# A two-layer hybrid decoder trunk on one core: the per-layer embedding's products and additions are set apart within an expert group's turn

## The chip, the cores and the metric

The kernel runs on one core of a Trainium2 chip. TensorE (PE in the profile; PEld is its weight load) multiplies, VectorE (DVE) and ScalarE (ACT) do the elementwise work and empty PSUM, GpSimd (POOL) does little here, and SyncE (SP) issues nearly all transfers. The metric is the device time of one execution in microseconds (us). Three runs of the kernel before took 963.85, 966.4 and 969.9 us; their median, 966.4 us, is the time before.

## The reference

Each of two layers has a token mixer (two kinds of attention) and a channel sublayer. Only the channel sublayer matters here. It works on 256 tokens of 1024 numbers in float32:

```
h   = silu(x W_g[e]) * (x W_u[e])            # 32 experts: 4 groups of 8, D_EXPERT = 256
moe = sum over a token's 2 experts of weight * (h W_d[e])
ple = sigmoid(x @ w_ple_gate) * (p @ w_ple)  # the per-layer embedding: 1024x1024 and 256x1024
x   = layer_norm(ALPHA * x + moe + ple)
```

The embedding `ple` doesn't depend on the experts. It only has to be added to the same sum before the layer norm.

## The kernel before

**The sum.** The output of the channel sublayer, 256 tokens by 1024 columns, stands in four PSUM banks for the whole stage: `ya[t][h]`, with t one of two halves of the tokens (128 each) and h one of two halves of the columns. The residual, the experts' results and the embedding are all added to it by matmuls of TensorE, so that nothing else reads or writes these banks until the layer norm. They are the tiles `acc` in the profile. Four more banks, `mm`, go round for everything else.

**The experts** are worked off in 11 groups (gi = 0 to 10), each of two or four experts whose tokens fill 128 slots in strips of 32. The loop at L1207 to L1231 runs over gi, and in one turn TensorE does, in this order:

- `front(gi + 1)` (L1126): the next group's gate and up products. For each of eight k there are four matmuls, one for each strip of 32 columns of the array, of 512 columns each (`mm<-a,a`, 128*32, in the profile; each matmul has two records, so a front has 32 matmuls and `x64`). ScalarE and VectorE make the activated product `sil` from it (`hidden_act`, L1049).
- `back(gi)` (L1141): this group's down products (`mm<-a,hT`). `halves_of` (L1063) splits them into two fp32r tiles, high by ScalarE (L208) and low by VectorE (L209).
- two gathers of the slots of group gi + 2 (`mm<-gs,a`), from marks that VectorE writes (`marks_of`, L929, one buffer);
- `turned` (L1055): the transposes of `sil` (`mm<-identr,sil`, L95);
- `combine` (L1068): eight matmuls that scatter this group's results into the four sums (`acc<-t,sT`);
- `embeds(gi)` (L1169), in the turns that have one;
- `ways_of` (L935): transposes of the marks (`mm<-identr,gs`) and the slots' weights (`mm<-cw,gs`). VectorE casts the transposes (L919) and copies the weights (L941).

The next turn's `front` follows.

**The embedding** is worked off in quarters of 256 columns (`Embed(q)`, q = 0 to 3) and halves of the tokens, eight units in a layer. One unit (`run(t)`, L741) has three steps:

- `products` (L746): eight matmuls of x and two of p into one `mm` bank, 128 by 256 each (`mm<-a,a` and `mm<-a,pT` with 128*128; two records each);
- `gate` (L759): ScalarE's sigmoid (L762), VectorE's product (L763), then the split into high (ScalarE, L208) and low (VectorE, L209);
- `add` (L768): two matmuls with the identity that add the high and the low part to `ya` (`acc<-t,identr`).

Turn 2 has both units of q = 0 (a part of the first one's products is done before), turns 4 and 5 both of q = 1 and q = 2, turn 6 the first of q = 3 and, in the second layer alone, also the second. In the first layer the last unit is made at the layer's end, by other lines. So 15 of 16 units stand in these turns.

**What sets the order.** The body of the loop is recorded with TensorE's order kept by hand (`manual_schedule`, L1211); the other engines' order comes from a scheduler. Every engine works its instructions off in their order. Weights come by DMA in tiles of 512 KB into an arena of 47 places; SyncE issues each one as soon as its place is free, in a fixed order, far ahead of use.

In turn 3 every engine also reads a count and passes a branch that isn't taken (`leftover`, L1187, in the profile as L1191).

Of the kernel before, what the change touches and what calls it, by code (L numbers as in the profile page):

```python
# [23 lines left out]
DEPTH = 2  # L24
P = 128
KT = D // P
TT = S // P
# [54 lines left out]
def tile_hybrid_trunk(ctx: ExitStack, tc: tile.TileContext, x_in, xT_in, pT_in, pos_in, ws, wik, wrt, lnv,  # L82
# [41 lines left out]
    def bank():  # L124
        return ps.tile([P, 512], F32, tag="mm", bufs=4, name=nm("mm"))

    def wt(shape, dt, tag, bufs):
        return wk.tile(shape, dt, tag=tag, bufs=bufs, name=nm(tag))
# [3 lines left out]
    class Held:  # L132


        def __init__(self, shape, dt=F32, load=False, place=None):
            self.b = arena.take(load, young) if place is None else place
            self.t = wk.tile([P, 1024], dt, tag=f"a{self.b}", bufs=1, name=nm("a"))
            if len(shape) == 2:
                names = "a b"
                self.v = self.t[:, :shape[0] * shape[1]].rearrange("p (a b) -> p a b", a=shape[0])  # L140
            else:
                self.v = self.t[:, :shape[0]]

        def free(self):
            arena.give(self.b)
# [16 lines left out]
    def load(l, i, shape):  # L162
        r = Held(shape, load=True)
        nc.sync.dma_start(r.t, ws[l, i])
        return r
# [19 lines left out]
    def t2(shape, dt=F32):  # L185
        return wt(shape, dt, "t2", t2b)
# [20 lines left out]
    def split(hi, lo, src, eng=V):  # L207
        copied[0] = A.activation(hi, src, AF.Copy)  # L208
        copied[1] = eng.tensor_tensor(lo, src, hi, op=OP.subtract)  # L209
# [124 lines left out]
    def proj(l, first, nk, xs, apart=0, ahead=(), ready=()):  # L334


        o = [acc() for _ in range(TT)]
        late = []

        def mm(t, kt, w):  # L340
            mm3(o[t], xs.get(kt, t), w.v[:, 0, :], w.v[:, 1, :], kt == 0, kt == nk - 1)

        for s in range(nk // 2):
            if not ready:
                r = ahead[s] if s < len(ahead) else load(l, first + s, [2, 512])
            for kt in (2 * s, 2 * s + 1):
                if ready:
                    w = ready[kt]
                elif kt < nk - apart or not ring:
                    w = parts(r.v[:, kt % 2, :], ring if kt < nk - apart else None)  # L350
                else:
                    w = parts(r.v[:, kt % 2, :], [ring.pop(0)])
                mm(0, kt, w)
                if kt < nk - apart:
                    mm(1, kt, w)
                else:
                    late.append((kt, w))
            if not ready:
                r.free()
        for kt, w in late:  # L360
            mm(1, kt, w)
            w.free()
        return o
# [89 lines left out]
    for l in range(DEPTH):  # L453
# [183 lines left out]
        def gate(h, i):  # L637
            g = Held([TT, 512])
            o = proj(l, 28 + 8 * i + 4 * h, KT, xT)
            for t in range(TT):  # L640
                A.activation(g.v[:, t, :], o[t], AF.Sigmoid)
            return g
# [89 lines left out]
        class Embed:  # L732


            def __init__(self, q):
                self.q = q
                self.w = [load(l, O_PLG + 2 * q + k4, [4, 256]) for k4 in range(2)]
                if q % 2 == 0:
                    wple[q // 2] = load(l, O_PLE + q // 2, [4, 256])

            def run(self, t):  # L741
                self.products(t)
                self.gate()
                self.add(t)

            def products(self, t, some=range(KT + 2)):  # L746
# [9 lines left out]
                        PE.matmul(b[:, 256:], pT[:, k - KT, ts], wple[q // 2].v[:, 2 * (q % 2) + k - KT, :], start=False,  # L756
                                  stop=k == KT + 1)

            def gate(self):  # L759
                b = self.b  # L760
                g = wt([P, 256], F32, "sil", silb)
                A.activation(g, b[:, :256], AF.Sigmoid)  # L762
                V.tensor_tensor(g, g, b[:, 256:], op=OP.mult)  # L763
                e = t2([P, 2, 256], F32R)
                split(e[:, 0, :], e[:, 1, :], g)
                self.e = e

            def add(self, t):  # L768
                q, e = self.q, self.e
                yq = ya[t][q // 2][:, (q % 2) * 256:(q % 2 + 1) * 256]  # L770
                for i in range(2):
                    PE.matmul(yq, identr, e[:, i, :], start=False, stop=False)
                if t == TT - 1:
                    free(*self.w)
                    if q % 2:
                        wple[q // 2].free()
# [6 lines left out]
        emb = {0: Embed(0)}  # L783
# [107 lines left out]
        def experts(gi):  # L891

            c = 0
            for r, n, w in groups[gi]:
                for i in range(n):
                    yield r + i, slice(c, c + w)
                    c += w

        def gather(gs, xg, k4):

            b = bank()
            for k in range(4):
                ks = slice((4 * k4 + k) * P, (4 * k4 + k + 1) * P)
                for t in range(TT):
                    PE.matmul(b[:, k * P:(k + 1) * P], x[t].v[:, ks], gs[:, t, :], start=t == 0, stop=t == TT - 1)
            A.activation(xg, b.rearrange("p (k s) -> p k s", k=4), AF.Copy)  # L906
# [28 lines left out]
        def ways_of(gi, gs):  # L935

            sT = wt([P, TT, P], F32R, "sT", 2)
            bw = ways(gs, [cw[:, :, r:r + n] for r, n, w in groups[gi]], sT)
            wsl = wt([P, 1], F32, "wsl", 3)
            for i, (r, sl) in enumerate(experts(gi)):  # L940
                V.tensor_copy(wsl[sl], bw[sl, i:i + 1])  # L941
            return sT, wsl
# [125 lines left out]
        def combine(y, sT, h, t, stop=False):  # L1068

            PE.matmul(ya[t][h], sT[:, t, :], y[0], start=False, stop=False)  # L1070
            PE.matmul(ya[t][h], sT[:, t, :], y[1], start=False, stop=stop)
# [97 lines left out]
        def embeds(gi):  # L1169

            if gi == e1:
                emb[0].products(0, range(wE, KT + 2))
                emb[0].gate()
                emb[0].add(0)
            if gi == e0:
                emb[0].run(1)
            if gi in early:
                q = 1 + early.index(gi)
                if q not in emb:
                    emb[q] = Embed(q)  # L1180
                emb[q].run(0)
                if q < 3:
                    emb[q].run(1)
            if gi == lastat and (l == DEPTH - 1 or lastemb == 2):
                emb[3].run(1)

        def leftover(most):  # L1187
            def onward(cols, n):
# [19 lines left out]
        for gi in range(len(groups)):  # L1208
            if gi == ifat:
                most = nc.values_load(cmi[0:1, 0:1], min_val=0, max_val=S)  # L1210
            here = lambda: tc.manual_schedule(engines={mybir.EngineType.PE})  # L1211
            with here():
                after = front(gi + 1, *slots) if gi < last else None
            if gi == ifat:
                leftover(most)
            with here():
                ys = back(gi, hT)
                if gi + 2 <= last:
                    marks, slots = marks_of(gi + 2), Gathered(gi + 2 >= fg)
                    for k4 in range(2):  # L1220
                        gather(marks, slots.half[k4], k4)
                if gi < last:
                    hT = turned(after[0], wt([P, 2 * P], F32, "hT", hTb))
                    for h in range(2):
                        for t in range(TT):
                            combine(ys[h], sT, h, t)
                    sT = after[1]
                embeds(gi)
                if gi + 2 <= last:
                    slots = slots, *ways_of(gi + 2, marks)  # L1230
            if gi == last - 1:  # L1231
                lng, lnb = wide(2, l), wide(3, l)
                xn = [Held([D]) for _ in range(TT)]
                if l < DEPTH - 1:
                    xT = Split(KT)
# [12 lines left out]
        for t in range(TT):  # L1248
            if t == 1 and l < DEPTH - 1 and lastemb < 2:
                with behind(ends[0] if f1 else None):  # L1250
                    emb[3].gate()
                emb[3].add(1)
            for h in range(2):
                combine(ys[h], sT, h, t, True)
            if t == 0 and l < DEPTH - 1 and lastemb < 2:
                emb[3].products(1)
            with behind((ysplit[1] if o3 else None) if t == 0 else (copied[1] if order2 else None)):
                power = norm.stats(t)
            ends.append(power)
            ends[t:] = [norm.apply(t, o2)]  # L1260
            powers.append(power)
# [76 lines left out]
```

## Time and profile before

| | |
|---|---|
| median of three runs | 966.4 us (963.85 to 969.9) |
| the profiled execution's own time | 968.06 us |
| its span, first to last instruction | 966.5 us |
| mean granted clock of TensorE | 0.987 |
| busy: PE, PEld | 94%, 63% |
| busy: DVE, ACT, POOL | 44%, 36%, 3% |
| transfers | 280.86 MB, mean 291 GB/s |

Busy shares are of the span. A line of the profile names the source line of the helper that records an operation (all matmuls are L92, all transposes by TensorE L95), so operations are told apart by their tiles. The idle time in front of an operation is that of its own engine, with what ended it.

### The profile page before, as it was taken

How to read it: one execution, taken by the hardware profiler on the slowest of the kernel's cores; microseconds unless marked ns; L12 is line 12 of the kernel's file. 1: busy time of each engine (PE TensorE's matmuls, PEld its weight loads, DVE VectorE, ACT ScalarE, POOL GpSimd, SP SyncE). 2: the span in 40 equal slices, each digit the busy share in tenths (PEclk: the TensorE clock that was granted, in tenths of full speed). 3: DMA queues.
4: the chain of work that ended last, by engine and by line, in shares of the span. 5: the costliest groups of instructions: out<-in, count | busy, mean ns of one | idle time of the engine just before them, and what ended most of it. 6: DMA issues, size and time to landing. Idle time of an engine off the chain costs nothing. (4 is left out here: it accounts for less than half of the span.)

```text
span 966.5 us, 15937 instructions
## 1 busy us (share of the span) xinstructions
PE 911.4 (94%) x5761; PEld 605.7 (63%) x5761; DVE 427.8 (44%) x1068; ACT 347.7 (36%) x704; POOL 33.3 (3%) x37
## 2 busy tenths in 40 slices
PE   8999999999998988999799999999999989888994
PEld 5877777785545466544488777787754646456441
DVE  6796566873121211122468864778622121211123
ACT  6557586522111111112346667765121111111120
POOL 0000000100000000000400000001000000000000
PEclk9999999999999999999999999999999999999998
DMA  8994335767899999795997243456869999979933
GB/s 298 408 417 161 125 110 179 261 244 284 320 360 415 388 417 376 310 416 234 397 418 306 88 131 131 139 196 235 305 215 372 378 409 415 399 299 408 370 144 145
DMA packets 79013, 280.86 MB, mean 291 GB/s; under 512 B 9160, under 2 KB 9928, under 8 KB 78928
## 3 DMA queue, kind: packets, MB, share of 16 engines
q1 hardware_dynamic: 78784, 279.78, 76.0%
q8 instruction: 47, 0.77, 0.3%
q14 instruction: 38, 0.31, 0.1%
q10 hardware_dynamic: 144, 0.00, 0.0%
HBM read 278.70 MB, written 1.05 MB: 289 GB/s over the span
## 5 line engine op out<-in xcount | busy, mean ns | idle before, releaser
L92 PE MATMUL acc<-a,a 128*128 128x512 f32 x1440 | 353.2, 399 | 2.1 <-ACT a L208 1.3
L92 PEld LDWEIGHTS acc<-a,a 128*128 128x128 f32 x1440 | 266.0, 189 | 65.1 <-issue 3.2
L92 PE MATMUL mm<-a,a 128*32 128x512 f32 (+5 forms) x1776 | 235.1, 537 | 0.0
L208 ACT ACTIVATE a<-a 128x512 fp32r<-128x512 f32 (+1 forms) x247 | 150.6, 631 | 99.9 <-PE acc L92 69.0
L209 DVE TENSOR_TENSOR a<-a,a 128x512 fp32r<-128x512 f32 (+1 forms) x239 | 161.0, 695 | 50.0 <-ACT a L208 48.6
L92 PEld LDWEIGHTS mm<-a,a 128*32 128x32 f32 (+3 forms) x1776 | 110.7, 132 | 101.4 <-issue 91.1
L92 PE MATMUL mm<-a,hT 128*32 128x512 f32 x704 | 92.2, 604 | 9.0 <-DMA a<-ws 5.0
L92 PEld LDWEIGHTS mm<-gs,a 128*128 128x128 f32 x704 | 80.4, 192 | 17.2 <-PE mm L92 11.7
L92 PE MATMUL mm<-gs,a 128*128 128x128 f32 x704 | 84.7, 278 | 0.0
L1050 ACT ACTIVATE sil<-mm 128x256 f32<-128x256 f32 x22 | 8.4, 383 | 183.2 <-PE mm L92 165.9
L92 PEld LDWEIGHTS mm<-a,hT 128*32 128x32 f32 x704 | 24.3, 111 | 71.5 <-issue 56.5
L1051 DVE SCALAR_TENSOR_TENSOR sil<-sil,wsl,mm 128x256 f32<-128x256 f32 x22 | 10.6, 481 | 131.4 <-ACT sil L1050 131.2
L209 DVE TENSOR_TENSOR t<-mm,t 128x512 fp32r<-128x512 f32 x44 | 30.4, 692 | 68.7 <-ACT t L208 68.7
L208 ACT ACTIVATE t<-mm 128x512 fp32r<-128x512 f32 x44 | 26.3, 597 | 79.0 <-PE mm L92 79.0
L763 DVE TENSOR_TENSOR sil<-sil,mm 128x256 f32<-128x256 f32 x16 | 6.7, 420 | 107.4 <-ACT sil L762 107.4
L92 PE MATMUL acc<-t,sT 128*128 128x512 f32 x176 | 48.8, 413 | 0.0
L906 ACT ACTIVATE a<-mm 128x512 f32<-128x512 f32 x40 | 23.9, 598 | 50.1 <-PE mm L92 50.1
L919 DVE CAST sT<-mm 128x256 fp32r<-128x256 f32 x22 | 9.3, 425 | 69.1 <-PE mm L92 69.1
L92 PEld LDWEIGHTS acc<-t,sT 128*128 128x128 f32 x176 | 31.4, 190 | 9.0 <-issue 2.5
L762 ACT ACTIVATE sil<-mm 128x256 f32<-128x256 f32 x16 | 6.1, 383 | 79.6 <-PE mm L92 79.6
L92 PE MATMUL acc<-t,identr 128*128 128x256 f32 x32 | 12.4, 388 | 21.8 <-ACT t L208 20.6
L548 ACT ACTIVATE t<-mm,mx 128x128 f32<-128x128 f32 (+1 forms) x64 | 26.0, 421 | 10.7 <-DVE mx L545 10.7
(197 smaller groups left out, 648.1 us busy)
## 6 DMA issues: line engine op xcount, KB each, us to landing
a<-ws SPq DMA_DIRECT2D x523, 512.0 KB, 8.4
a<-x_in SPq DMA_DIRECT2D x2, 512.0 KB
out<-a SPq DMA_DIRECT2D x4, 256.0 KB, 2.7
a<-xT_in SPq DMA_DIRECT2D x3, 256.0 KB
a<-wik SPq DMA_DIRECT2D x2, 288.0 KB, 7.6
a<-ws SPq DMA_DIRECT2D x2, 256.0 KB, 4.2
pT<-pT_in SPq DMA_DIRECT2D x2, 256.0 KB
a<-wrt SPq DMA_DIRECT2D x2, 144.0 KB, 2.8
```

What stands on the lines that cost most here:

```text
L92: self.last = nc.tensor.matmul(*a, **k)
L208: copied[0] = A.activation(hi, src, AF.Copy)
L209: copied[1] = eng.tensor_tensor(lo, src, hi, op=OP.subtract)
L548: A.activation(e[:, i * nk:(i + 1) * nk], b[:, i * nk:(i + 1) * nk], AF.Exp, bias=mx[:, i:i + 1], accum_out=sums[i])
L762: A.activation(g, b[:, :256], AF.Sigmoid)
L763: V.tensor_tensor(g, g, b[:, 256:], op=OP.mult)
L906: A.activation(xg, b.rearrange("p (k s) -> p k s", k=4), AF.Copy)
L919: V.tensor_copy(sT, b[:, :2 * P].rearrange("p (t q) -> p t q", t=TT))
L1050: A.activation(sil, gu[:, :FE], AF.Sigmoid)
L1051: V.scalar_tensor_tensor(sil, sil, wsl, gu[:, :FE], op0=OP.mult, op1=OP.mult)
```

## The change

`embeds(gi)` no longer runs the units. It returns a list of them, and the loop calls their three steps at different places of the turn: the first unit's products ahead of `turned`, its gate after `combine`, then the second unit's products and gate, then `ways_of`, and both additions last. `Embed` keeps the gated tiles by t, since two of them are alive now.

```diff
             def __init__(self, q):
-                self.q = q
+                self.q, self.e = q, {}
...
             def run(self, t):
                 self.products(t)
-                self.gate()
+                self.gate(t)
                 self.add(t)
...
-            def gate(self):
+            def gate(self, t):
...
-                self.e = e
+                self.e[t] = e
 
             def add(self, t):
-                q, e = self.q, self.e
+                q, e = self.q, self.e.pop(t)
...
         def embeds(gi):
 
             if gi == e1:
-                emb[0].products(0, range(wE, KT + 2))
-                emb[0].gate()
-                emb[0].add(0)
-            if gi == e0:
-                emb[0].run(1)
+                return [(emb[0], 0, range(wE, KT + 2)), (emb[0], 1, range(KT + 2))]
+            units = []
             if gi in early:
                 q = 1 + early.index(gi)
                 if q not in emb:
                     emb[q] = Embed(q)
-                emb[q].run(0)
-                if q < 3:
-                    emb[q].run(1)
-            if gi == lastat and (l == DEPTH - 1 or lastemb == 2):
-                emb[3].run(1)
+                units = [(emb[q], t, range(KT + 2)) for t in range(TT if q < 3 else 1)]
+            if gi == lastat and l == DEPTH - 1:
+                units.append((emb[3], 1, range(KT + 2)))
+            return units
...
+                units = embeds(gi)
+                for e, t, some in units[:1]:
+                    e.products(t, some)
                 if gi < last:
                     hT = turned(after[0], wt([P, 2 * P], F32, "hT", hTb))
                     for h in range(2):
                         for t in range(TT):
                             combine(ys[h], sT, h, t)
                     sT = after[1]
-                embeds(gi)
+                for e, t, _ in units[:1]:
+                    e.gate(t)
+                for e, t, some in units[1:]:
+                    e.products(t, some)
+                    e.gate(t)
                 if gi + 2 <= last:
                     slots = slots, *ways_of(gi + 2, marks)
+                for e, t, _ in units:
+                    e.add(t)
```

What this does to TensorE's order is shown for turn 4 of the first layer. Here are its rows before, from the last matmul of `combine` on (`mm_3368` and `mm_3387` are the banks of the two units' products, `acc_2072` and `acc_2074` the sums to which they are added, `mm_3407` is `ways_of`, `mm_3453` the front of group 6):

```order
L92 MATMUL acc_2075<-t_640_3329,sT_2856 128x512
L92 MATMUL mm_3368<-a_2309,a_2069 128x256 x4
L92 MATMUL mm_3368<-a_2311,a_2070 128x256 x4
L92 MATMUL mm_3368<-a_2082,pT_1485 128x256 x2
L92 MATMUL acc_2072<-t_649_3382,identr 128x256 x2
L92 MATMUL mm_3387<-a_2309,a_2069 128x256 x4
L92 MATMUL mm_3387<-a_2311,a_2070 128x256 x4
L92 MATMUL mm_3387<-a_2082,pT_1485 128x256 x2
L92 MATMUL acc_2074<-t_652_3401,identr 128x256 x2
L95 MATMUL mm_3407<-identr,gs_3332 128x128 x2
L92 MATMUL mm_3407<-cw_2177,gs_3332 128x2 x2
L92 MATMUL mm_3453<-a_3428,a_3334 32x512 x2
```

Here are TensorE's rows of the change from the same place on (the first unit's products, now `mm_3355`, stand ahead of `turned` and `combine` and so above these rows; the second unit's are `mm_3385`, `ways_of` is `mm_3403`):

```order
L92 MATMUL acc_2075<-t_640_3329,sT_2852 128x512
L92 MATMUL mm_3385<-a_2309,a_2069 128x256 x4
L92 MATMUL mm_3385<-a_2311,a_2070 128x256 x4
L92 MATMUL mm_3385<-a_2082,pT_1485 128x256 x2
L95 MATMUL mm_3403<-identr,gs_3332 128x128 x2
L92 MATMUL mm_3403<-cw_2177,gs_3332 128x2 x2
L92 MATMUL acc_2072<-t_649_3382,identr 128x256 x2
L92 MATMUL mm_3453<-a_3428,a_3334 32x512 x2
L92 MATMUL mm_3453<-a_3439,a_3334 32x512 x2
L92 MATMUL mm_3453<-a_3428,a_3334 32x512
L92 MATMUL acc_2074<-t_652_3399,identr 128x256 x2
L92 MATMUL mm_3453<-a_3428,a_3334 32x512
```

Each addition stood right behind its unit's products. Now the first unit's stands behind `ways_of`, and the second unit's stands in the next group's front, after five of its 32 matmuls: four of k = 0 and the first of k = 1. All eight first units and all seven second units of the two layers stand so.

On VectorE the second unit's gate and `ways_of` are interleaved in the change. Its rows for the same turn are these (`sil_3379` and `t_649_3382` belong to the first unit, `sil_3396` and `t_652_3399` to the second, `gs_3535` are the marks of a later group):

```order
L763 TENSOR_TENSOR sil_3379<-sil_3379,mm_3355 128x256
L209 TENSOR_TENSOR t_649_3382<-sil_3379,t_649_3382 128x256
L919 CAST sT_3402<-mm_3403 128x256
L763 TENSOR_TENSOR sil_3396<-sil_3396,mm_3385 128x256
L941 COPY wsl_3409<-mm_3403 64x1 x2
L929 TENSOR_TENSOR gs_3535<-iom,posm_2178 128x256
L209 TENSOR_TENSOR t_652_3399<-sil_3396,t_652_3399 128x256
```

The low half of the second unit (the last row) stood ahead of the cast, the copies and the marks before, and stands behind them now. Turn 5 has four copies in place of two, and turn 2 no marks at this place. SyncE's transfers keep their order, but two of them pass to the other side of the branch of turn 3.

## Rows read from the trace of the kernel before

**Rows 1.** The page's first part: busy time of the engines.

```profile
PE 911.4 (94%) x5761; PEld 605.7 (63%) x5761; DVE 427.8 (44%) x1068; ACT 347.7 (36%) x704; POOL 33.3 (3%) x37
```

**Rows 2.** The page's costliest groups: xcount | busy, mean ns | idle before, releaser.

```profile
L92 PE MATMUL mm<-a,hT 128*32 128x512 f32 x704 | 92.2, 604 | 9.0 <-DMA a<-ws 5.0
...
L92 PE MATMUL acc<-t,identr 128*128 128x256 f32 x32 | 12.4, 388 | 21.8 <-ACT t L208 20.6
```

**Rows 3.** Timeline, first layer, turn 4: start, length, operation, idle before it.

```profile
341.82 0.38 PE L95 MATMUL mm<-identr,sil 128*128 128x128 f32 x2
341.96 2.10 PE L92 MATMUL acc<-t,sT 128*128 128x512 f32 x8
...
343.90 3.61 PE L92 MATMUL mm<-a,a 128*128 128x256 f32 x16
347.35 1.03 PE L92 MATMUL mm<-a,pT 128*128 128x256 f32 x4
348.41 0.38 ACT L762 ACTIVATE sil<-mm 128x256 f32<-128x256 f32 x1 [5.52 <-PE mm L92]
348.83 0.42 DVE L763 TENSOR_TENSOR sil<-sil,mm 128x256 f32<-128x256 f32 x1 [9.20 <-ACT sil L762]
349.28 0.42 ACT L208 ACTIVATE t<-sil 128x256 fp32r<-128x256 f32 x1 [0.49 <-DVE sil L763]
349.73 0.43 DVE L209 TENSOR_TENSOR t<-sil,t 128x256 fp32r<-128x256 f32 x1 [0.48 <-ACT t L208]
349.75 0.85 PE L92 MATMUL acc<-t,identr 128*128 128x256 f32 x2 [1.38 <-ACT t L208]
350.44 3.62 PE L92 MATMUL mm<-a,a 128*128 128x256 f32 x16
...
353.90 1.03 PE L92 MATMUL mm<-a,pT 128*128 128x256 f32 x4
...
356.30 0.85 PE L92 MATMUL acc<-t,identr 128*128 128x256 f32 x2 [1.38 <-ACT t L208]
356.98 0.38 PE L95 MATMUL mm<-identr,gs 128*128 128x128 f32 x2
357.20 0.51 PE L92 MATMUL mm<-cw,gs 128*128 128x2 f32 x4
...
357.74 0.42 DVE L919 CAST sT<-mm 128x256 fp32r<-128x256 f32 x1 [1.04 <-PE mm L92]
358.08 0.32 DVE L941 COPY wsl<-mm 64x1 f32<-64x1 f32 x2
358.43 0.43 DVE L929 TENSOR_TENSOR gs<-iom,posm 128x256 f32<-128x256 f16 x1
```

**Rows 4.** Timeline of TensorE: five fronts or backs, in both layers.

```profile
316.03 5.34 PE L92 MATMUL mm<-a,hT 128*32 128x512 f32 x32 [2.09 <-DVEq L1191]
...
387.56 8.77 PE L92 MATMUL mm<-a,a 128*32 128x512 f32 x64
...
412.63 7.07 PE L92 MATMUL mm<-a,a 128*32 128x512 f32 x64
...
831.89 8.64 PE L92 MATMUL mm<-a,a 128*32 128x512 f32 x64
...
893.41 8.60 PE L92 MATMUL mm<-a,a 128*32 128x512 f32 x64
```

**Rows 5.** Timeline of TensorE, first layer, last group's back and combine.

```profile
458.30 1.04 PE L92 MATMUL mm<-a,hT 128*32 128x512 f32 x2
459.27 0.97 PE L92 MATMUL acc<-t,sT 128*128 128x512 f32 x3
```

**Rows 6.** Stretches of 20 us: busy time of PE, PEld, DVE, ACT, POOL; granted clock, DMA share, GB/s.

```profile
380.00:400.00 20.00, 18.48 (x128) 8.56 (x128) 3.90 (x12) 1.92 (x5) 0.00 (x0) 0.91 0.65 242
```

**Rows 7.** Timeline of SyncE, first layer: one run of weight transfers issued.

```profile
355.28 84.21 SPq L1040 DMA_DIRECT2D a<-ws  x62
```

**Rows 8.** The page's transfers: KB each, median us from issue to landing.

```profile
a<-ws SPq DMA_DIRECT2D x523, 512.0 KB, 8.4
```

More of the change, by code (lines that the diff above doesn't have):

```diff
@@ L1250, in tile_hybrid_trunk @@
                 with behind(ends[0] if f1 else None):
-                    emb[3].gate()
+                    emb[3].gate(1)
                 emb[3].add(1)
```

## Prediction, made before the changed kernel ran

> **What bounds the kernel now.** I read the busy times first: TensorE has 94% of the span, VectorE 44% [rows 1]. So the end is set by TensorE's work and by its own waits, and a change is worth what it does to these. Next the page's groups, for idle time in front of TensorE's operations. The largest is 21.8 us ahead of the 32 matmuls that add the embedding; 20.6 of it ended with ScalarE's split [rows 2]. Then the timeline of one turn that has two units [rows 3]: the products end at 347.35 + 1.03 = 348.38, and TensorE stands still until 349.75 while the unit's own sigmoid, product and high half (348.41 to 349.70) are made one after the other. The second unit repeats this to the hundredth: 1.38 each, and 15 x 1.38 = 20.7 is the 20.6 of the group. So it is a latency, with nothing else to do in TensorE's order, and not a busy ScalarE or VectorE.
>
> **The waits removed.** The whole price of one is more than 1.38, because the second addition also waits, for VectorE's low half. From the first unit's first product to the second's is 350.44 - 343.90 = 6.54 us. Sixteen records of such products start 347.35 - 343.90 = 3.45 apart, 0.216 each; so 20 records take 4.31, and two additions at the same pace 0.43. The rest, 6.54 - 4.31 - 0.43 = **1.80 us**, is wait. For 15 units: 27.0 us.
>
> For the eight first units I take all of it. Their gate needs about 1.8 us from the products' end (348.38 to 349.73 + 0.43); between them and their addition now lie the transposes, `combine` (341.82 to 343.90, 2.1 us), the second unit's products (4.3) where there is one, and `ways_of` (356.98 to 357.71 at most). If that cover went, the wait of 1.80 would be back. Their products ahead of `combine` delay nothing that is near its use: what `turned` writes is wanted a front later. Gain: 8 x 1.80 = 14.4.
>
> **The second units' addition in the next front.** It is late enough, by this count from the end E of their products. Sigmoid from E + 0.03. The cast starts 0.76 after the first transpose of `ways_of` (356.98 to 357.74), and this now starts 0.16 ahead of E, as in an unbroken stream; so cast at E + 0.60. Cast to the end of the marks took 1.12 (357.74 to 358.86), and the gate's product of 0.42 stands between: to E + 2.14. The low half ends at E + 2.57, with four copies some 0.33 later. TensorE reaches the place after 0.65 for `ways_of`, 0.43 for the first unit's addition, four matmuls of the front (0.88, an eighth of 7.07 [rows 4]) and one alone. This one has a near row: at the end of the first layer a single strip matmul stands ahead of full-array ones, and from its start to theirs pass 459.27 - 458.30 = 0.97 us [rows 5]. So the place comes at E - 0.16 + 0.65 + 0.43 + 0.88 + 0.97 = E + 2.77 for the high and about E + 2.98 for the low half, against 2.57 to 2.90: no wait, or 0.1.
>
> But the 0.97 is a price. In a front four strips share the array, and a matmul's share is 7.07 / 32 = 0.22. When one of the four goes alone, the other three take as long as the four did. I take **1.0 us** for each of seven, from that row. Bounds: nothing, if the profile's row owes its length to something else and the three are quicker for it; 1.5, if going back to strips costs another half microsecond. Second units therefore gain 7 x (1.80 - 1.0) = 5.6.
>
> The Trainium skill (TensorEngine Tiling, Key Properties) says that changing the tiling mode drains TensorE. That rule speaks against this place, which changes the mode twice. Row and rule agree that the change of mode costs; but a drain alone would be the 0.97 less the matmul's own 0.88, some 0.1 each way, and the sum would then be lower by 7 x 0.8 = 5.6 us, 938.
>
> **The clock.** Two fronts of the second layer and one of the first, each right behind two such waits, took 8.77, 8.64 and 8.60 instead of 7.07 [rows 4]; around the first the granted clock was 0.91 [rows 6], 1.2 GHz in place of 2.4 for a part of it. That is 1.70 + 1.57 + 1.53 = 4.8 us. The same two waits at 349 and 356 had no such front behind them, so the waits are not enough by themselves. Without them TensorE has no stop in these turns, and I take the 4.8 as given back. The back after the branch (5.34 [rows 4]) has its own wait of 2.09, which stays; I leave it. Bounds: nothing back, or 1.7 more.
>
> **Other queues.** The weights must come earlier by what TensorE gains, at most 12 to 13 us a layer. In the first layer the last of 62 transfers is issued at 355.28 + 84.21 = 439.49 [rows 7], lands some 8.4 later [rows 8], at 447.9, and the place where such a last tile is used is at 458.30 [rows 5]: 10 us ahead. The transfers also have room, with a share of 0.65 at 380 to 400 [rows 6], where they waited for places that TensorE now frees sooner. So they move up, and cost nothing. The two transfers that pass the branch wait for no more than before.
>
> **Sum.** 14.4 + 5.6 + 4.8 = 24.8 us, against the profiled execution's 968.06: **943.3 us**. That execution stood 1.7 above the median of the runs; I give 943, and the range allows for it.
>
> **Rivals.**
> - *The clock is no better.* As many slow fronts as before, here or elsewhere: 968.06 - 20.0 = 948. For it: the same waits are without a slow front at 349 and 356, and the lone strip leaves most of the array unused. Against it: all three followed the waits. The Trainium skill (TensorE: Matmul & The Clock Gate, Why this matters for your kernels) lays falls of the clock to idle gaps longer than these 1.38 us. By that rule the waits are not the cause, and this rival holds; the slow fronts right behind them speak against it. Chance 0.22.
> - *The broken front is dearer,* 1.5 us and a wait of 0.5 for the low half, which now stands behind cast, copies and marks in VectorE's order: the second units give nothing, 27.0 - 14.0 + 4.8 = 17.8, so 950. Chance 0.10.
> - *The weights come late.* If none could move up, the first layer's gain (4 x 1.80 + 3 x 0.80 + 1.7 = 11.3) would meet the lead of 10.4 (458.30 - 447.9) and lose 0.9; the second's, 13.5, taken with the same lead, 3.1: 947. Speaking for it, 5.0 us of TensorE's idle ended with such a transfer already [rows 2]; none of it in these turns. Chance 0.06.
> - *Slower.* Place: the second units' addition in the front, with everything of that front behind it. If VectorE were held at the cast, copies or marks, all of TensorE would stand. The change loses from 24.8 / 7 = 3.5 us more at each, and is slower by 1% from (24.8 + 9.7) / 7 = 4.9; at 6 us it would be 985. Against it, nothing in that stretch of VectorE waits for what TensorE does behind the addition, and its four operations sum to 1.6 us. Chance 0.02.
> - *It doesn't do what it says:* the waits only move to other places of the turn, within 1% of before, 963. Against it stands the order, with several us of work in every gap. Chance 0.03.
>
> My forecast has the remaining 0.57. The range goes from 937 (the lone strip nearly free, 27.0 + 4.8 = 31.8 less) to 953 (a dearer front at 1.5 us and the clock no better: 968.06 - 27.0 + 10.5 = 951.6, and some more). About 1%, 9.7 us, can be told from no change; all cases but the last two lie beyond it on the fast side: faster 0.93, same 0.04, slower 0.03.
>
> **What would show it.** In the profile after: no idle time ended by ScalarE's split ahead of `acc<-t,identr` but for crumbs; about 4.3 us from products to whatever follows; a front with a second unit that lasts some 1.4 us longer (1.0 and the two additions); fronts of 7.07 behind the turns 4, 5 and 6; no new waits for weights. It would be wrong if a front waits for VectorE's low half, if the slow fronts are still there, or if TensorE's gaps come back as waits for `ws`.

## The result and the profile after

The changed kernel takes **940.68 us** (median of four runs, 938.6 to 944.42), the kernel before in the same comparison 968.15 (963.85 to 969.9). The ratio is 0.9727 with an interval of 0.9679 to 0.9774: 2.7% faster. The profiled execution takes 940.85 us with a span of 939.2, against 968.06 and 966.5 before. The mean granted clock rose from 0.987 to 0.994.

The busy times of the page, the answer to [rows 1]:

```profile
PE 906.3 (96%) x5761; PEld 604.4 (64%) x5761; DVE 425.7 (45%) x1068; ACT 347.9 (37%) x704; POOL 33.8 (4%) x37
```

TensorE is busy 5.1 us less with as many instructions, and its span is 27.3 us shorter. So about 22 us less of it is idle and 5 us less busy. These two are not the waits and the clock: the busy time before also holds the second additions' waits for the low half (0.85 us for two additions in [rows 3], 0.48 or 0.50 below), and the busy time after holds what the broken fronts cost. Of the groups of [rows 2] the second has left the page: no addition of the embedding waits for ScalarE in any turn. The first stands as it was, 4.9 us of waits for weights in place of 5.0:

```profile
L92 PE MATMUL mm<-a,hT 128*32 128x512 f32 x704 | 96.4, 603 | 8.8 <-DMA a<-ws 4.9
```

This is the timeline of turn 4 of the first layer, the answer to [rows 3] (start, length, operation; the idle time before it in brackets):

```profile
339.50 3.62 PE L92 MATMUL mm<-a,a 128*128 128x256 f32 x16
342.95 1.03 PE L92 MATMUL mm<-a,pT 128*128 128x256 f32 x4
...
343.95 2.10 PE L92 MATMUL acc<-t,sT 128*128 128x512 f32 x8
345.90 3.61 PE L92 MATMUL mm<-a,a 128*128 128x256 f32 x16
349.35 1.03 PE L92 MATMUL mm<-a,pT 128*128 128x256 f32 x4
350.21 0.38 PE L95 MATMUL mm<-identr,gs 128*128 128x128 f32 x2
350.41 0.38 ACT L762 ACTIVATE sil<-mm 128x256 f32<-128x256 f32 x1 [5.04 <-PE mm L92]
...
350.79 0.48 PE L92 MATMUL acc<-t,identr 128*128 128x256 f32 x2
...
351.21 1.90 PE L92 MATMUL mm<-a,a 128*32 128x512 f32 x10
...
351.76 0.42 ACT L208 ACTIVATE t<-sil 128x256 fp32r<-128x256 f32 x1 [0.96 <-DVE sil L763]
...
352.33 0.42 DVE L209 TENSOR_TENSOR t<-sil,t 128x256 fp32r<-128x256 f32 x1
353.04 0.50 PE L92 MATMUL acc<-t,identr 128*128 128x256 f32 x2
353.47 5.78 PE L92 MATMUL mm<-a,a 128*32 128x512 f32 x51
...
363.05 3.84 PE L92 MATMUL mm<-gs,a 128*128 128x128 f32 x32
```

The reader is to see three things. The products at 339.50 end at 342.95 + 1.03 = 343.98, and 6.8 us of other work lie between them and their addition at 350.79. The second unit's halves are ready at 352.18 (high, 351.76 + 0.42) and 352.75 (low), and TensorE takes them up at 353.04, so nothing waits. And the front is in two pieces, with ten records (five matmuls) ahead of that addition: from its start to the gathers that follow the back pass 363.05 - 351.21 = 11.84 us. Turn 6 of the first layer has one unit, and the front behind it is whole:

```profile
401.34 7.07 PE L92 MATMUL mm<-a,a 128*32 128x512 f32 x64
408.23 3.62 PE L92 MATMUL mm<-a,hT 128*32 128x512 f32 x32
411.78 3.84 PE L92 MATMUL mm<-gs,a 128*128 128x128 f32 x32
```

That is 411.78 - 401.34 = 10.44 us from front to gathers, so the broken front costs 1.40: two additions of 0.216 each, 0.43, and **0.97** for the matmul that goes alone.

Whole turns are best measured from the first gather of one to the first of the next, since these rows are alike in both kernels. Turn 4 of the first layer began at 335.82 above and lasts 27.23 us. Before, it lasted 29.92:

```profile
338.15 3.84 PE L92 MATMUL mm<-gs,a 128*128 128x128 f32 x32
...
368.07 3.84 PE L92 MATMUL mm<-gs,a 128*128 128x128 f32 x32
```

All turns with units, read in this way (us; turn 6 of the first layer has one unit, the others two; a star marks a turn with one of the three slow fronts of [rows 4]):

| | layer 1: turn 2 | 4 | 5 | 6 | layer 2: turn 2 | 4 | 5 | 6 |
|---|---|---|---|---|---|---|---|---|
| before | 32.64 | 29.92 | 31.63* | 23.37 | 30.71 | 31.56* | 29.92 | 31.56* |
| after | 29.89 | 27.23 | 27.22 | 21.51 | 28.00 | 27.22 | 27.22 | 27.23 |
| less | 2.75 | 2.69 | 4.41 | 1.86 | 2.71 | 4.34 | 2.70 | 4.33 |

Their sum is 25.8 us of the 27.3. Another 1.4 lies between the layers, where the change moves nothing. TensorE stops there twice in both kernels, and before, the operations behind the stops then ran slower (first fence, before; second, after):

```profile
479.66 0.66 PE L95 MATMUL mm<-identr,a 128*128 128x128 f32 x4 [0.89 <-DVE a L414]
480.04 1.14 PE L92 MATMUL acc<-a,a 128*128 128x512 f32 x2
...
483.11 4.31 PE L92 MATMUL acc<-a,a 128*128 128x512 f32 x17
```

```profile
468.17 0.63 PE L95 MATMUL mm<-identr,a 128*128 128x128 f32 x4 [0.88 <-DVE a L414]
468.55 0.71 PE L92 MATMUL acc<-a,a 128*128 128x512 f32 x2
...
470.25 4.13 PE L92 MATMUL acc<-a,a 128*128 128x512 f32 x17
```

The same operations take 483.11 - 480.04 = 3.07 us before and 470.25 - 468.55 = 1.70 after. The granted clock of the stretch from 475 to 485 was 0.83 before (columns as in [rows 6]), 1.2 GHz for a part of it, and 1.00 in the one from 465 to 475 after:

```profile
475.00:485.00 10.00, 7.70 (x32) 5.97 (x31) 8.61 (x13) 2.06 (x5) 8.78 (x8) 0.83 1.03 419
```

```profile
465.00:475.00 10.00, 7.82 (x40) 6.05 (x40) 9.82 (x14) 1.91 (x4) 8.68 (x7) 1.00 1.02 419
```

This 1.4 is not shown to belong to the change. Of the ten traces only that of the kernel before is slow there. The same operations take 1.70 us in that of the filled waits and 1.72 in that of the second units as before (both below), though the first has the order of the kernel before and the second seven of its waits.

The slow back behind the branch [rows 4] is still there, with the stop that it had:

```profile
313.73 5.31 PE L92 MATMUL mm<-a,hT 128*32 128x512 f32 x32 [2.09 <-DVEq L1187]
```

### The profile page after: what moved, and what is told of

Same layout as the page of the kernel before. It is cut to its first block, busy times and chain, and to the rows that moved or that the text cites. A ratio compares the mean times of both kernels' runs of the same rounds, so it can differ in the third digit from the quotient of the medians.

```text
span 939.2 us, 15942 instructions
## 1 busy us (share of the span) xinstructions
PE 906.3 (96%) x5761; PEld 604.4 (64%) x5761; DVE 425.7 (45%) x1068; ACT 347.9 (37%) x704; POOL 33.8 (4%) x37
## 3 DMA queue, kind: packets, MB, share of 16 engines
HBM read 278.70 MB, written 1.05 MB: 298 GB/s over the span
## 5 line engine op out<-in xcount | busy, mean ns | idle before, releaser
L92 PE MATMUL mm<-a,a 128*32 128x512 f32 (+5 forms) x1776 | 237.6, 526 | 0.0
L92 PE MATMUL mm<-a,hT 128*32 128x512 f32 x704 | 96.4, 603 | 8.8 <-DMA a<-ws 4.9
L383 POOL PARTITION_BROADCAST a<-a x8 | 10.6, 1356 | 511.0 <-DMA a<-lnv 279.6
```

Source lines behind the costliest of these rows:

```text
L92: self.last = nc.tensor.matmul(*a, **k)
L383: G.partition_broadcast(r.v, r.v[0:1])
```

## The experiments

My theory after the result had four parts: each wait that went was worth 1.8 to 1.9 us; the matmul that goes alone is dear because its three companions of the group of four go later in a round of their own; the slow fronts came from the waits; and the transfers had lead enough. The rivals were that the 0.97 is a price of changing the array's tiling (a drain), that the clock fell for another reason, and that part of the gain came from elsewhere.

**The additions between two groups of four** (timed in three rounds). The second units' additions are placed behind eight of the next front's 32 matmuls, where two rounds of four are complete (`done` frees the unit's weights, which `add` did before).

```diff
-                for e, t, _ in units:
+                for e, t, _ in units[:1]:
                     e.add(t)
+                for e, t, _ in units[1:]:
+                    late.append((e, t))
+                    e.done(t)
...
             def front(gi, ...):
...
+                if kt == 1:
+                    while late:
+                        e, t = late.pop(0)
+                        e.add(t, True)
```

> The second units' additions stand in the next front after eight of its 32 matmuls (the end of k = 1), not after five; all else as in the change. Theory (a strip matmul that goes alone costs 0.97 us because the other three then take as long as four): from the front's start to the first gather behind its back 10.44 + 0.43 for the two additions = 10.87 us in the seven turns, where the change has 11.84 (351.21 to 363.05 in turn 4 of the first layer); 7 x 0.97 = 6.8 us less in all, about 934 us. Rival (the price is that of changing between strips and the full array, wherever it is done): 11.8 as in the change, 941 us. If the gate is not ready at the new place, an idle time ended by ScalarE's or VectorE's split stands ahead of the addition; by the trace of the change it is ready 0.3 us earlier.

It took 934.49 us (932.43 to 937.22), ratio to the kernel before 0.9656 [0.9624, 0.9689]. The profile's span is 934.9. Turn 4 of the first layer, again:

```profile
352.39 1.92 PE L92 MATMUL mm<-a,a 128*32 128x512 f32 x16
354.24 0.50 PE L92 MATMUL acc<-t,identr 128*128 128x256 f32 x2
354.68 5.36 PE L92 MATMUL mm<-a,a 128*32 128x512 f32 x48
...
363.40 3.84 PE L92 MATMUL mm<-gs,a 128*128 128x128 f32 x32
```

The front is still in two pieces, but the turns 4 to 6 with two units last 26.39 or 26.40 us in place of 27.22, and the two turns 2 last 29.10 and 27.17: 0.79 less in the one with the slow back, 0.83 or 0.84 in the other six. The tiling still changes twice here, and from the front's start to the gathers pass 363.40 - 352.39 = 11.01 us, 0.14 more than the 10.87 of a whole front with two additions. So of the 0.97 the round that is not full makes 0.83, and the two changes of tiling 0.14. The rival that the price is a drain falls, and this version is faster than both kernels.

**Two and two instead of one and three** (one run). The additions stand behind six matmuls, so that neither piece of the second group of four is a lone matmul.

```diff
+                for n, (i, sl) in enumerate(strips(gi)):
+                    while late and kt == 1 and n == 2:
+                        e, t = late.pop(0)
+                        e.add(t, True)
```

> As the kernel with the additions after eight matmuls, but after six: two strips of k = 1 before, two behind. Theory (when the four strips are parted, each part takes as long as the four would): the price is the same as for one and three, 0.83 us more for a turn than at a boundary; from gather to gather 27.2 in the turns with two units, in all 7 x 0.83 = 5.8 us more, 940. Rival (the price lies in the one strip that goes alone): less than half of that, 26.4 to 26.8 a turn, 935 to 937.

It took 938.07 us; the turns with two units (4 to 6) are 27.22 or 27.23 again.

```profile
348.41 1.91 PE L92 MATMUL mm<-a,a 128*32 128x512 f32 x12
350.25 0.50 PE L92 MATMUL acc<-t,identr 128*128 128x256 f32 x2
350.68 5.77 PE L92 MATMUL mm<-a,a 128*32 128x512 f32 x50
```

Six matmuls take 1.91 us, as the eight of the experiment ahead take 1.92 and the five of the change 1.90. So rounds are what counts. Front and back have 32 and 16 matmuls, 12 rounds of four; parted behind five or six, the pieces need 2 and 11 rounds (43 and 42 matmuls are 10.75 and 10.5 rounds), one more than unparted; behind eight they need 2 and 10.

**The additions behind the first group of four** (one run). Behind four matmuls there is no split group either, but VectorE's low half may not be ready.

```diff
+                if kt == 0:
+                    while late:
+                        e, t = late.pop(0)
+                        e.add(t, True)
```

> As the kernel with the additions after eight matmuls, but after four, the first boundary. It measures the gate's length as the prediction counted it: the low half ready 2.57 us after the products' end (2.90 with four copies), the place for it reached at about 2.0. Theory: an idle time of about 0.1 for the high and 0.4 to 0.8 for the low half ahead of the additions, and the turn longer by the same, 26.9 to 27.2 in place of 26.4. Rival (the gate is quicker than counted, as VectorE and ScalarE overlap): no wait, 26.4.

It took 937.38 us. In turns 4 to 6 the scheduler pulled one matmul of a back into the gap, so that these turns had a lone matmul again and took 27.21 to 27.23; they don't answer the question. (So TensorE's order is by hand only within a piece of the program: where front and body meet, the scheduler can move a matmul, as it did in the change when it put an addition that the program names ahead of the front behind five matmuls of it.) Turn 2 answers it, in both layers alike; these are rows of the first:

```profile
302.24 1.06 PE L92 MATMUL mm<-a,a 128*32 128x512 f32 x8
303.25 0.85 PE L92 MATMUL acc<-t,identr 128*128 128x256 f32 x2
```

```profile
303.23 0.42 DVE L209 TENSOR_TENSOR t<-sil,t 128x256 fp32r<-128x256 f32 x1 [0.25 <-ACT t L208]
```

The pair of additions lasts 0.85 in place of 0.50, since its second half is written until 303.65. So the place behind four comes too early, by less than half a microsecond, and only for the low half, though in turn 2 no marks stand ahead of it on VectorE; at five (the change) nothing waited.

**The waits filled** (one run). The kernel before, with ten small matmuls of bf16 into a free bank ahead of each pair of additions: the waits are covered, and nothing else moves. The products of these matmuls are not used.

```diff
             def add(self, t):
...
+                if not (q == 3 and t == 1 and l < DEPTH - 1):
+                    b = bank()
+                    for _ in range(10):
+                        PE.matmul(b[:, :256], identb, cmb, start=True, stop=True)
                 for i in range(2):
                     PE.matmul(yq, identr, e[:, i, :], start=False, stop=False)
```

> The kernel before, with ten matmuls of the identity into a spare bank ahead of each of the 15 pairs of additions: they fill TensorE's wait for the gate and change nothing else (their result is not used). Theory (the slow fronts behind turns 4, 5 and 6 came from the waits): the additions come no earlier, 15 waits of 1.80 us are still in the time, but the three slow fronts (8.77, 8.64, 8.60 us) take 7.07; 968 less 4.8, about 963 us, and no fall of the granted clock in those turns. Rival (where the clock falls is chance, or hangs on something else of these turns): three or more slow fronts again, 968 us.

It took 961.83 us, with a span of 960.2. Here is turn 5 of the first layer, which had the front of 8.77:

```profile
386.12 1.26 PE L92 MATMUL mm<-cmb,identb 128*128 128x256 bf16 x10
387.66 0.85 PE L92 MATMUL acc<-t,identr 128*128 128x256 f32 x2 [0.28 <-ACT t L208]
...
389.00 7.07 PE L92 MATMUL mm<-a,a 128*32 128x512 f32 x64
```

The additions come no earlier than before, and the idle time ahead of each is 0.28 or 0.29 instead of 1.38. The three turns with a star in the table now last 29.92, 29.92 and 29.93, as their neighbours do. The order is that of before, and only what TensorE does in the waits differs. One run alone doesn't show that the waits brought the clock down: seven runs of the kernel before on the same chip took 965.01 to 969.61 us at a granted clock of 0.985 to 0.989, and this one stands below them at 0.994, but on another chip the kernel before itself had runs of 961.15 and 962.63 at 0.994 and 0.993, with all its waits. The traces together say more. In the two with waits of 1.38 us (the kernel before and the next experiment) six of the 15 fronts behind such waits are slow; in the eight others no front behind units is, 64 in all. So the waits are the likely cause, and by themselves not enough.

**The second units as before** (one run). Only the first units are set apart; the second ones are added right behind their products.

```diff
                 for e, t, some in units[1:]:
                     e.products(t, some)
                     e.gate(t)
+                    e.add(t)
...
-                for e, t, _ in units:
+                for e, t, _ in units[:1]:
                     e.add(t)
```

> The change for the first units alone: the second unit's addition stands right behind its products and its gate again, ahead of ways_of. Theory: seven waits of 1.80 us come back and seven broken fronts at 0.97 go: +7 x 0.83 = 5.8 us against the change, about 947, with 1.38 idle ahead of each such addition. On the clock the theory is open: one wait of 1.38 a turn is half of what the kernel before had; if slow fronts come back, 1.6 us more for each. Rival (the second units gain nothing by the change, since what the wait cost is paid in the front): 941, as the change.

It took 948.87 us. Of the turns 4 to 6, those without a slow front last 28.04 to 28.05 in place of 27.22 (turns 4 and 5 of the first layer and 6 of the second), so a second unit set apart is worth 0.83 in the change. The kernel before took 29.92 in such turns where no front was slow, so a first unit set apart is worth 1.87. In three of the seven turns with two units the front was slow again, each behind one wait of 1.38 (8.62 us in turn 2 of the first layer, 8.34 and 8.77 in turns 4 and 5 of the second). This is turn 4 of the second layer:

```profile
814.71 0.85 PE L92 MATMUL acc<-t,identr 128*128 128x256 f32 x2 [1.38 <-ACT t L208]
...
816.75 8.34 PE L92 MATMUL mm<-a,a 128*32 128x512 f32 x64
```

So it needn't be two waits in a turn. Why it was these three and not the other four is not to be read from the trace.

**The first units' products back behind `combine`** (one run).

```diff
                 units = embeds(gi)
-                for e, t, some in units[:1]:
-                    e.products(t, some)
...
-                for e, t, _ in units[:1]:
+                for e, t, some in units[:1]:
+                    e.products(t, some)
                     e.gate(t)
```

> The change, but the first unit's products stand behind combine again, where they were before; gates and additions as in the change. Theory (what pays is that the addition is apart from the gate; early products are needed only where no second unit stands between): turns with two units as in the change, since the second unit's products (4.3 us) cover the first gate; turn 6 of the first layer, with one unit, waits some 1.1 us again (1.80 less 0.65 for the work of ways_of). In all +1.1 us, about 942. Rival (the early products are the main part, since they fill a wait ahead of the transposes or the combine): the gain of the first units is lost in part, 947 to 955.

It took 942.53 us. The turns with two units stayed at 27.22: the second unit's products and `ways_of` are cover enough for the first one's gate. Turn 6 of the first layer, which has one unit, went from 21.51 to 22.56. I had expected 1.1, but from a wait. The trace shows none:

```profile
400.47 1.90 PE L92 MATMUL mm<-a,a 128*32 128x512 f32 x10
402.30 0.50 PE L92 MATMUL acc<-t,identr 128*128 128x256 f32 x2
```

The addition was put behind five matmuls of the front, and the 1.05 is once more about the price of a broken front. A right number with a wrong reason: `combine` as cover is needed only where a turn has one unit.

**Twelve of the 47 places for weights kept empty** from turn 1 to the start of turn 9 (one run; the rest as in the first experiment).

```diff
         for gi in range(len(groups)):
+            if gi == 1:
+                idle = [Held([D]) for _ in range(12)]
+            if gi == last - 1:
+                free(*idle)
```

> As the kernel with the additions after eight matmuls, but twelve of the 47 places of the weights are kept empty from turn 1 to turn 9 of each layer. It tests how far the transfers are from being the bound. A place holds 512 KB, 1.25 us of transfer at the full rate of 418 GB/s seen in the trace. Theory (the weights of the last group land 7 to 8 us ahead of their use in the first layer, some 11 in the second): 12 x 1.25 = 15 us less lead, so 4 to 8 us of new waits for ws in each layer, 942 to 950. Rival (the transfers are far from it, since they only wait for free places): no new waits, 934 to 936.

It took 954.03 us, 19.5 more than the first experiment and past what I had expected. Turns 2 to 6 lasted as in that one. The front and the back of the last group stopped for weights:

```profile
428.87 2.10 PE L92 MATMUL acc<-t,sT 128*128 128x512 f32 x8
...
444.03 1.04 PE L92 MATMUL mm<-a,hT 128*32 128x512 f32 x2 [0.15 <-DMA a<-ws]
445.29 1.04 PE L92 MATMUL mm<-a,hT 128*32 128x512 f32 x2 [0.22 <-DMA a<-ws]
...
454.41 1.41 PE L92 MATMUL acc<-t,sT 128*128 128x512 f32 x5
```

```profile
420.00:440.00 20.00, 19.54 (x148) 9.25 (x140) 3.30 (x10) 3.05 (x6) 0.00 (x0) 1.00 1.03 418
```

From one combine to the next pass 25.5 us, against 13.2 in the first experiment; in the second layer 21.7, against 13.2. The transfers fill the stretch ahead of it: a DMA share of 1.03 and 418 GB/s, at which a tile of 512 KB takes 1.25 us, and TensorE's pairs of records follow each other at 1.26. The idle times in brackets show little of it, 0.15 to 0.22 each. So the lead over the weights is not large: with a quarter of the places gone, more than half of the first experiment's gain is lost. Whether the kernel before would lose as much without them no run shows.

**The branch's stop filled** (timed in three rounds). The first experiment, with the second unit of turn 2 moved to turn 3: its products stand between the front and the branch, its gate in the program behind the branch (the order of ScalarE and VectorE is the scheduler's).

```diff
             if gi == e1:
-                return [(emb[0], 0, range(wE, KT + 2)), (emb[0], 1, range(KT + 2))]
+                return [(emb[0], 0, range(wE, KT + 2))]
...
                 after = front(gi + 1, *slots) if gi < last else None
+                if gi == ifat:
+                    emb[0].products(1)
...
+                if gi == ifat:
+                    emb[0].gate(1)
...
+                if gi == ifat:
+                    emb[0].add(1)
```

> As the kernel with the additions after eight matmuls (934.5 us), but the second unit of turn 2 goes to turn 3: its products stand between the front and the branch of turn 3, its gate behind the branch, its addition behind ways_of of turn 3. Theory (TensorE's stop at the branch, 2.1 and 1.9 us in the two layers, is a wait for other engines that work on the front's result, and work can lie beside it): 4.0 us of waits go, and with them the slow back behind the branch in the first layer (5.3 in place of 3.6): 5.7 less, about 929. Rival (the stop is the branch's own price on TensorE, its load of the count and its jump): it stands behind the products just as long, and the time is 934 to 935, with a slow back or without.

It took 933.62 us (932.12 to 936.23), ratio 0.9682 [0.964, 0.9724]: no difference from the first experiment that the runs can show, and not the 929 that I expected.

```profile
310.97 1.03 PE L92 MATMUL mm<-a,pT 128*128 128x256 f32 x4
312.03 0.38 ACT L762 ACTIVATE sil<-mm 128x256 f32<-128x256 f32 x1 [4.07 <-PE mm L92]
312.45 0.42 DVE L763 TENSOR_TENSOR sil<-sil,mm 128x256 f32<-128x256 f32 x1 [3.52 <-ACT sil L762]
313.46 3.64 PE L92 MATMUL mm<-a,hT 128*32 128x512 f32 x32 [1.47 <-DVEq L1197]
```

The products at 310.97 stand right ahead of the branch, and TensorE still stops for 1.47 us, where it stopped for 2.09; in the second layer for 1.25 in place of 1.88. This does not make it the branch's own price. The moved unit's sigmoid and product ran ahead of the branch on ScalarE and VectorE, so VectorE was late at the branch again, this time for the unit: its own branch instruction starts at 313.1. What let TensorE go on is named as VectorE's queue at the branch (DVEq L1197), and TensorE goes on 0.59 us after VectorE's last operation ahead of it (313.46 against 312.45 + 0.42), as in the first experiment (314.89 against 313.88 + 0.42):

```profile
313.88 0.42 DVE L1058 TENSOR_TENSOR sil<-sil,mm 128x256 f32<-128x256 f32 x1
...
314.89 5.34 PE L92 MATMUL mm<-a,hT 128*32 128x512 f32 x32 [2.10 <-DVEq L1197]
```

In the second layer it is 0.37 in both. So all of the stop but these last 0.59 or 0.37 us is a wait for VectorE's work, as the theory had it, and the experiment did not take that wait away. A unit whose gate stays behind the branch on every engine was not tried, and what the 0.59 and 0.37 consist of is open. The back behind the branch ran at full pace here, but it did so behind stops of 2.05 to 2.10 in three of the other experiments too, so the shorter stop is not shown to be the reason.

## Why the prediction was right, point by point

- **The first units, 8 x 1.80 = 14.4.** Right, and slightly small. The turn with one unit, which has no broken front, saved 1.86, and a first unit beside a second one 1.87 (29.92 - 28.05). By that the eight make 14.9.
- **The second units, 7 x (1.80 - 1.0) = 5.6.** The forecast's price for the lone matmul was 1.0, the measured one 0.97, and a front with a second unit lasts 1.40 longer, as it said. Setting them back cost 0.83 a turn where no front was slow, which is 1.80 for the wait less 0.97, and 7 x 0.83 = 5.8. The mechanism, that three take as long as four, was right and could be separated: 0.83 for the round, 0.14 for the two changes of tiling.
- **No wait for the low half.** Right, with 0.29 us to spare (352.75 against 353.04), where the prediction had between none and 0.1 of wait. From the products' end at 350.38 the low half took 2.37 us, where 2.57 had been counted, and the place came after 2.66, where it was 2.77. One matmul less ahead of it, and there was a wait.
- **The clock, 4.8.** Right in size: beyond the 2.7 us of its neighbours, a turn with a slow front saved 1.6 to 1.7, together 4.41 + 4.34 + 4.33 - 3 x 2.7 = 5.0. Filling the waits gave the same in one run without moving anything, and no front was slow in any trace without the waits; that they are the cause is likely by this. The turns without a star show that a wait does not always have a slow front behind it. That the size came out is in part luck: in 14 runs of the kernel before, the granted clock lay between 0.985 and 0.994 and the time between 961.15 and 969.71, so what the clock takes differs from run to run, and the 4.8 was read from a single one.
- **Weights, no cost.** Right: waits for them are 4.9 us after and 5.0 before. But the lead was used up in part, and the room in the transfers too: the DMA share from 380 to 400 is 1.03 after, where it was 0.65. The last of the 62 transfers of the first layer is issued at 352.78 + 77.98 = 430.76 (row below), lands some 9.4 us later (the median of the page after) at 440.2, and the place that the prediction took for its use is now at 446.99: some 7 us ahead, in place of 10. The experiment on places shows that this was a matter of lead, not of course.

```profile
352.78 77.98 SPq L1040 DMA_DIRECT2D a<-ws  x62
```

- **What was missed.** The 1.4 us between the layers. The prediction did not look for slow stretches outside the turns, and that this one was in the trace before and not in the one after is luck of the two runs as far as is known. Of the 2.5 by which the spans fell more than its 24.8, this is 1.4; the steps' sizes make 1.0 (25.8 for the turns against 24.8), half of it in the first units' waits, and 0.1 is elsewhere.

The steps as measured sum to 14.9 + 5.8 + 5.0 = 25.7, and the turns show 25.8.

The rival *the clock is no better* fell. The Trainium skill (TensorE: Matmul & The Clock Gate, Why this matters for your kernels) speaks for it, as the prediction said; here six of 15 fronts behind waits of 1.38 us were slow and none without them, so the measurement speaks against that rule for this kernel. The Trainium skill's other rule, that a change of tiling mode drains TensorE (TensorEngine Tiling (Array Packing), Key Properties), agrees with the trace as far as the two changes cost 0.14 us; that this is a drain no run shows. By the two changes alone the second units' gain would have come out some 5.6 us higher by the prediction's count, which the first experiment got and the change did not. *The broken front is dearer* fell by the 0.97 and the absent wait; *the weights come late* by the equal waits for them; *slower* and *doesn't do what it says* by the turns' lengths. The range's lower end, 937, is 936 by its own sum (968.06 - 31.8).

Open is which waits bring the clock down, and why it fell between the layers in one trace and in none of the others. The second of the two stops there is 0.88 or 0.89 us in every trace; the first is 1.41 in that of the kernel before, and 0.51 to 1.28 in the others. Open is the slow back behind the branch too: it stands in six of the nine traces with a stop of 2.05 to 2.18 us. Not tried was a front whose parted place is chosen for each turn.

## What to carry to other kernels

A wait for a short chain on other engines goes when the work that follows is put between the producer and the consumer; before that, count the chain from start to end, with what now stands ahead of it in the other engines' order. Work that is put into a stream of strip matmuls belongs between full rounds: two extra matmuls there cost 0.14 us more than their own time, and inside a round 0.97. And look at the operations behind a wait as well as at the wait: three slow fronts gave a fifth of this gain in the profiled pair, and filling the waits got them back in the one run of it.

## What the runs showed of the hardware

- Behind TensorE's waits of 1.38 us, one or two in a turn, six of 15 fronts took 8.34 to 8.77 us instead of 7.07, with the granted clock at 1.2 GHz for a part (0.91 over 380 to 400 us in the kernel before, 1.00 with the waits filled to 0.28); the other nine did not, and none of 64 fronts in the traces without such waits.
- Four strip matmuls make a round of about 0.87 us (10.44 / 12), and a round that is not full takes as long: 1.90, 1.91 and 1.92 us for five, six and eight matmuls.
- Two changes between strips and the full array cost 0.14 us (11.01 against 10.87).
- At a branch that isn't taken TensorE stopped until VectorE had come to it: it went on 0.59 us after VectorE's last operation ahead of the branch in the first layer, 0.37 in the second, with stops of 2.10 and 1.88 us as with 1.47 and 1.25.
